# Layer 1's feed-forward: the second half's norm steps and the down weights' splits at other products of a tile

## The chip, the core and the metric

One core of a Trainium2 chip runs the whole program. The metric is the device time of one execution in microseconds. In the profile PE is the matrix engine (TensorE), DVE VectorE, ACT ScalarE, POOL GpSimd, and SP the engine that here only issues DMA transfers.

## What is computed

A two-layer block over 1024 latent tokens and 256 context tokens of width 1024, in float32. Layer 0 mixes by Fourier groups and windowed attention, layer 1 by neighbourhood attention; each layer ends with a SwiGLU feed-forward. Cut to the part that matters here, layer 1's end:

```
o = _neighbourhood_attention(q, k, v, kc, vc, rel_bias) @ w_out
x = x + g1 * o
h = _rms(x, norm2_g[i]) * (1.0 + sc2) + sh2
x = x + g2 * ((jax.nn.silu(h @ wg) * (h @ wu)) @ wd)     # D_FF = 2816
```

## The kernel before

Every float32 product is made of three matmuls on parts: an operand is split into a high part (rounded) and a low part (the rest), and `mm3` (lines 74 to 76) adds high x high, high x low and low x high. ACT makes a high part by a copy, POOL or DVE the low part by a subtraction. These splits, not only the matmuls, fill the other engines.

Layer 1's feed-forward works on two halves of 512 tokens. The 2816 hidden columns are 22 tiles of 128 (`NF`), so there are 44 tiles (`NT1`): n = 0 to 21 for the first half, 22 to 43 for the second. In a tile the gate and up products are computed together as seven block products (`p`, s = 0 to 6, lines 1451 to 1495) over four combinations of the weights' blocks; `sums1` makes the combinations on POOL (tile `t`, line 1400), `high1` and `low1` split them (lines 1413, 1417, 1425), five to seven products ahead of their use. DVE and ACT combine the seven results (lines 1466 to 1484), ACT makes `act_hi` (line 1489) and POOL `act_lo` (line 1492). Products with the down weights (`d`, `down_product`, line 1497) take two tiles' `act` at once: eight of them, for tiles n and n+1 with n even, stand four in tile n+2 and four in tile n+3, behind s = 2, 4, 5 and 6. The order of all these items is a list, `items`, and on PE, DVE, ACT and POOL every instruction runs in the order of the program (`manual_schedule`). SP is not in that list; its order is chosen by the compiler's planner.

The input of a half is normed ahead of its tiles. For the first half this is done by `norm0s` during the out projection. For the second half `norm1s` (a generator, line 1300) does it during the tiles of the first half: each `advance(own1, 1)` runs it to its next `yield`. It makes eight squares on ACT (line 1308) with sums on POOL (line 1309), a chain by two groups of small matmuls with Ln and Exp between them (lines 1313 to 1322), and then, for four pairs of columns blocks, `own` tiles: a product on POOL (line 1327) and a scale on ACT (1328) for each of the two, differences on POOL (1330 to 1334), and four pieces that are split by ACT (`own_hi`, 1339) and POOL (1340) and leave by DMA for the buffer `c_d` in HBM. `own_hi` has one buffer. In tile 21 the parts come back from `c_d` on SP's queue, and tile 22 reads them.

`split_down(n, h, t)` splits half h of the down weights of tile n: t = 0 is ACT's copy (line 1444), t = 1 POOL's subtraction (line 1446). `load_down(n + 1)` at s=5 of tile n loads both halves into `wd_raw`, which has three buffers (line 1436). What steps run behind which product is written out at the end of the loop over `items`.

Of the kernel before, what the change touches and what calls it, by code (L numbers as in the profile page):

```python
# [27 lines left out]
NF = DFF // P  # L28
# [27 lines left out]
def bc(ap, axis, n):  # L56

    ap = ap.unsqueeze(axis)
    shape = list(ap.shape)
    shape[axis] = n  # L60
    return ap.broadcast_to(shape)


def build(tc, io):
    nc = tc.nc
# [3 lines left out]
    def fl(ap):  # L69
        return ap.bitcast(F32)  # L70
# [7 lines left out]
    def rsqrt_into(r, v, tmp):  # L78

        S.activation(r, v, AF.Ln)  # L80
        S.activation(r, r, AF.Exp, scale=-0.5)
        V.tensor_tensor(tmp, r, r, ALU.mult)
        V.scalar_tensor_tensor(tmp, v, -0.5, tmp, ALU.mult, ALU.mult)
        V.scalar_tensor_tensor(r, tmp, 1.5, r, ALU.add, ALU.mult)
# [27 lines left out]
    def vec(l, which):  # L112
        return mod[l][:, which * KT:(which + 1) * KT, :]
# [36 lines left out]
    def advance(steps, n):  # L150

        for _ in range(n):
            if next(steps, steps) is steps:
                return
# [90 lines left out]
    def product(c, u, k, out, c0, n):  # L245
        ts = slice(u * P, u * P + P)
        mm3(out, hs[c][0][:, k, ts], hs[c][1][:, k, ts], w_hi[:, k, c0:c0 + n], w_lo[:, k, c0:c0 + n],
            k == 0, k == KT - 1)
# [100 lines left out]
    for c in range(T // CH):  # L349
        h_hi, h_lo = hs[c]  # L350

        for u in range(CH // P):
# [34 lines left out]
            for i, h0, nh in ((0, 0, 8), (1, 8, 2)):  # L387
                src = pqf[:, h0 * HD:(h0 + nh) * HD]
# [83 lines left out]
    for half in range(2):  # L472
# [5 lines left out]
        for gg in range(2):  # L478
# [3 lines left out]
            for i0, parts in ((0, (0, 4)), (2, (1, 2)), (4, (3,))):  # L482
# [8 lines left out]
                n = len(parts)  # L491
                src = ps[:, 0:n].rearrange("p n r l -> p r n l")
# [25 lines left out]
    for grp in range(4):  # L518
# [5 lines left out]
        src = ps.rearrange("p n r l -> p r n l")  # L524
# [703 lines left out]
    HT = 256  # L1228
# [71 lines left out]
    def norm1s():  # L1300

        ss = wk.tile([P, 512], F32, name="nrm_ss")
        for k in range(KT):
            if k == 0:
                S.activation(ss, x[:, k, 512:], AF.Square)
            else:
                sq = wk.tile([P, 512], F32, name="nrm_sq", tag="nrm_r")
                S.activation(sq, x[:, k, 512:], AF.Square)
                G.tensor_tensor(ss, ss, sq, ALU.add)
            yield  # L1310
        ps = ph.tile([P, 512], F32, name="pmisc")
        for j in range(4):
            TE.matmul(ps[:, j:j + 1], ss[:, j * P:(j + 1) * P], ones[:, 0:1], start=True, stop=True)
        v = wk.tile([P, 3, 4], F32, name="nrm_v", bufs=2)
        S.activation(v[:, 0], ps[:, :4], AF.Identity, bias=eps, scale=1.0 / D)
        rsqrt_into(v[:, 1], v[:, 0], v[:, 2])
        yield
        ps = ph.tile([P, 512], F32, name="pmisc")
        for j in range(4):
            TE.matmul(ps[:, j * P:(j + 1) * P], bc(v[:, 1, j], 1, P), ident, start=True, stop=True)  # L1320
        r = wk.tile([P, 512], F32, name="nrm_r")
        S.copy(r, ps)
        yield
        for i in range(4):
            h0, h4, s_, r_ = (wk.tile([P, 512], F32, name="own", bufs=4) for _ in range(4))
            for k, h in ((i, h0), (i + 4, h4)):
                G.tensor_tensor(h, x[:, k, 512:], r, ALU.mult)  # L1327
                S.activation(h, h, AF.Identity, bias=vec(1, 3)[:, k, 0:1], scale=nA[3][:, k, 0:1])  # L1328
                yield
            G.tensor_tensor(s_[:, M1], h0[:, M2], h4[:, M2], ALU.add)  # L1330
            G.tensor_tensor(s_[:, M2], s_[:, M1], h0[:, M1], ALU.subtract)
            yield
            G.tensor_tensor(r_[:, M1], h0[:, M1], h0[:, M2], ALU.subtract)
            G.tensor_tensor(r_[:, M2], h4[:, M1], s_[:, M2], ALU.subtract)
            yield
            for sl, src in ((slice(0, 1), h0[:, M1]), (slice(1, 3), h4), (slice(3, 5), s_), (slice(5, 7), r_)):
                n = (sl.stop - sl.start) * HT
                hi = wk.tile([P, 512], F32R, name="own_hi", tag="nrm_ss")
                S.copy(hi[:, :n], src)
                G.tensor_tensor(src.bitcast(F32R), src, fl(hi[:, :n]), ALU.subtract)  # L1340
                yield
                for t, part in ((0, fl(hi[:, :n])), (1, src)):
                    nc.scalar.dma_start(c_d[:, sl, t, i], part.rearrange("p (a n) -> p a n", n=HT))
                yield


# [22 lines left out]
    NT1 = 2 * NF  # L1369
# [19 lines left out]
    def sums1(q):  # L1389

        n, s = divmod(q, 7)
        if n >= NT1:
            return
        d = tiles[n]
        b11, b12, b22, b21 = d["b"]
        which = {0: ("t1", b12, b11), 1: ("t2", b22, d.get("t1")), 2: ("t3", b22, b12), 4: ("t4", d.get("t2"), b21)}
        if s in which:
            name, a, b = which[s]
            d[name] = wk.tile([P, 4, P], F32, name=name, tag="t", bufs=4)
            G.tensor_tensor(d[name], a, b, ALU.subtract)  # L1400

    def high1(q):

        n, s = divmod(q, 7)
        if n >= NT1:
            return
        if s == 0 and n + 1 < NT1:
            load_tile(n + 1)
        d = tiles[n]
        b11, b12, b22, b21 = d["b"]  # L1410
        src = (b11, d.get("t2"), d.get("t3"), d["t1"], d.get("t4"), b21, b22)[s]
        hi, lo = (ww.tile([P, 4, P], F32R, name=m) for m in ("w_hi", "w_lo"))
        S.copy(hi, src)  # L1413
        first = fl(hi)
        if s < 6:
            first = ph.tile([P, 512], F32, name="pmisc").rearrange("p (k n) -> p k n", n=P)
            S.copy(first, fl(hi))  # L1417
        d["w"][s] = hi, lo, src, first

    def low1(q):  # L1420
        n, s = divmod(q, 7)
        if n >= NT1:
            return
        hi, lo, src, first = tiles[n]["w"][s]
        (V if s < 6 else G).tensor_tensor(lo, src, first, ALU.subtract)  # L1425
# [4 lines left out]
    c_d = tc.dram_tile([P, 7, 2, 4, HT], F32, name="c_d")  # L1430
    down_raw = {}

    def load_down(n):
        for h in range(2):
            raw = wk.tile([P, 4, P], F32, name="wd_raw", bufs=3)
            nc.sync.dma_start(raw, io["w_down"][1, n % NF][:, 4 * h:4 * h + 4])
            down_raw[n, h] = raw

    def split_down(n, h, t):

        f = n % NF
        parts = [w_room[n // 2 % 2][:, f % 2, h, i] for i in range(2)]
        if t == 0:
            S.copy(parts[0], down_raw[n, h])
        else:
            G.tensor_tensor(parts[1], down_raw.pop((n, h)), fl(parts[0]), ALU.subtract)  # L1446
# [50 lines left out]
    def down_product(n, dt):  # L1497
        ci, f = divmod(n, NF)
        w_in = w_room[n // 2 % 2]
        ts = slice(ci * 512, ci * 512 + 512)  # L1500
        ps = pd.tile([P, 512], F32, name="d_ps")
        for i in range(2):
            mm3(ps, w_in[:, i, dt // 4, 0, dt % 4], w_in[:, i, dt // 4, 1, dt % 4], *tiles[n + i]["act"],
                i == 0, i == 1)
        V.scalar_tensor_tensor(x[:, dt, ts], ps, vec(1, 5)[:, dt, 0:1], x[:, dt, ts], ALU.mult, ALU.add)  # L1505
        if f == NF - 2:
            nc.scalar.dma_start(io["out"][:, dt, ts], x[:, dt, ts])
# [18 lines left out]
    with tc.manual_schedule(engines={E.PE, E.DVE, E.Activation, E.Pool}):  # L1526
        for i, (kind, n, s) in enumerate(items):
            for step in later.pop(i, ()):
                step()
            if kind == "d":  # L1530
                down_product(n, s)
                continue
            q = 7 * n + s
            sums1(q + LEAD + 2)
            if q:
                low1(q + LEAD - 1)
            high1(q + LEAD)
            product(i, n, s)
            if s == 5 and n + 1 < NT1:
                load_down(n + 1)  # L1540
            if q == 0:
                load_down(0)
            if s in (3, 4):
                split_down(n, 0, s - 3)
            if s in (0, 1) and n:
                split_down(n - 1, 1, s)
            if n == NT1 - 1 and s > 4:
                split_down(n, 1, s - 5)
            if 0 < n < NF - 1 and s in (0, 2, 4, 6):
                advance(own1, 1)  # L1550
            if n == NF - 1:

                for t, dst in ((0, c_hi), (1, c_lo)):
                    nc.sync.dma_start(fl(dst[:, SLOTS[s]]), c_d[:, SLOTS[s], t])
        for i in sorted(later):
            for step in later[i]:
                step()
# [113 lines left out]
```

## Time and profile before

| | us |
|---|---|
| median of 3 runs | 2896.84 |
| lowest and highest of them | 2896.06 and 2900.75 |
| the profiled execution | 2901.23 |
| its span | 2899.4 |

The profiled execution is 4.4 us above the median of the runs, and 1.8 us of its time lie outside the span. In the timeline a line gives the start in us from the span's beginning, the duration, engine, line and operation, and in brackets the time the engine stood idle before it with what ended the wait. Matmuls overlap, so one of 0.28 us follows another after 0.12 us.

### The profile page before, as it was taken

The numbers are of one execution on the slowest core, as the hardware profiler recorded it, in microseconds if no ns is written. First come the engines' busy times: TensorE is split into PE (matmuls) and PEld (weight loads), VectorE is DVE, ScalarE is ACT, GpSimd is POOL, SyncE is SP. The second block draws the span as 40 slices with busy tenths as digits, with TensorE's granted clock in tenths as the row PEclk, the third lists the DMA queues.
The fourth block names the chain that finished last, engine by engine and source line by source line (L and its number), as shares of the span: only waits on it lengthen the run. The fifth ranks groups of instructions, "written<-read, shape, count | busy, mean of one in ns | idle before, by whom it ended". The sixth has DMA issues, their size and how long they took to land. (4 is left out here: it accounts for less than half of the span.)

```text
span 2899.4 us, 44678 instructions
## 1 busy us (share of the span) xinstructions
PE 2799.8 (97%) x16874; PEld 2346.2 (81%) x16874; DVE 1510.4 (52%) x3069; ACT 1214.7 (42%) x2402; POOL 825.3 (28%) x857
## 2 busy tenths in 40 slices
PE   7988999999999999999989999999998999999999
PEld 5876767888888888888867788777777888999998
DVE  5775553533223333333377243366556676666665
ACT  4345553421111111111154232466637677666664
POOL 1122332000000000000040000355427788666664
PEclk9988999999999999999999999999999999999999
DMA  7235655211011011011124333877354344363331
GB/s 281 76 125 215 220 217 160 73 37 41 33 37 44 30 44 44 30 44 36 38 87 137 104 109 110 197 180 167 95 163 137 113 133 144 106 240 103 105 103 70
DMA packets 162375, 321.10 MB, mean 111 GB/s; under 512 B 13904, under 2 KB 78928, under 8 KB 155120
## 3 DMA queue, kind: packets, MB, share of 16 engines
q1 hardware_dynamic: 147200, 294.05, 32.4%
q10 hardware_dynamic: 13008, 15.87, 1.5%
q0 software_dynamic: 1952, 8.32, 1.0%
q8 instruction: 134, 2.20, 0.3%
q14 instruction: 81, 0.66, 0.1%
HBM read 269.83 MB, written 48.37 MB: 110 GB/s over the span
## 5 line engine op out<-in xcount | busy, mean ns | idle before, releaser
L74 PE MATMUL p_ps<-c_hi,w_hi 128*128 128x256 f32 x1232 | 343.6, 279 | 3.1 <-ACT own L1328 1.5
L76 PE MATMUL p_ps<-c_hi,w_lo 128*128 128x256 f32 x1232 | 342.2, 278 | 1.6 <-DVE w_lo L1425 1.0
L75 PE MATMUL p_ps<-c_lo,w_hi 128*128 128x256 f32 x1232 | 342.1, 278 | 0.0
L810 POOL TENSOR_TENSOR nrm_ss<-nrm_ss,nrm_sq 128x512 f32<-128x512 f32 (+1 forms) x31 | 39.3, 1269 | 1011.9 <-PE d_ps L76 935.7
L775 ACT CAST w_hi<-w_raw 128x1024 fp32r<-128x1024 f32 x106 | 110.3, 1050 | 482.5 <-PE d_ps L75 270.5
L74 PEld LDWEIGHTS p_ps<-c_hi,w_hi 128*128 128x128 f32 x1232 | 233.0, 189 | 12.3 <-ACT pmisc L1417 1.5
L75 PEld LDWEIGHTS p_ps<-c_lo,w_hi 128*128 128x128 f32 x1232 | 232.9, 189 | 6.8
L76 PEld LDWEIGHTS p_ps<-c_hi,w_lo 128*128 128x128 f32 x1232 | 232.7, 189 | 2.2 <-DVE w_lo L1425 1.5
L580 POOL TENSOR_SCALAR pr<-pr,st 128x640 f32<-128x640 f32 (+2 forms) x208 | 156.7, 754 | 267.1 <-DVE st L579 177.3
L878 DVE SCALAR_TENSOR_TENSOR x<-d_ps,mod,x 128x512 f32<-128x512 f32 (+1 forms) x240 | 157.5, 661 | 125.3 <-PE d_ps L76 125.3
L776 DVE TENSOR_TENSOR w_lo<-w_raw,w_hi 128x1024 fp32r<-128x1024 f32 x102 | 124.1, 1223 | 183.3 <-ACT w_hi L775 180.9
L862 DVE TENSOR_TENSOR sg<-sg,u_ps 128x512 f32<-128x512 f32 (+1 forms) x66 | 39.5, 599 | 319.9 <-PE u_ps L76 319.9
L1505 DVE SCALAR_TENSOR_TENSOR x<-d_ps,mod,x 128x512 f32<-128x512 f32 x176 | 132.1, 751 | 127.0 <-PE d_ps L76 126.4
L74 PE MATMUL d_ps<-act_hi,w_hi 128*128 128x512 f32 (+1 forms) x528 | 189.3, 359 | 3.4 <-DVE x L878 3.4
L75 PE MATMUL d_ps<-act_lo,w_hi 128*128 128x512 f32 (+1 forms) x528 | 189.2, 358 | 1.3 <-DVE act_lo L864 1.3
L76 PE MATMUL d_ps<-act_hi,w_lo 128*128 128x512 f32 (+1 forms) x528 | 189.2, 358 | 0.0
L74 PE MATMUL u_ps<-o_hi,w_hi 128*128 128x512 f32 (+1 forms) x528 | 188.3, 357 | 0.0
L75 PE MATMUL u_ps<-o_lo,w_hi 128*128 128x512 f32 (+1 forms) x528 | 188.3, 357 | 0.0
L76 PE MATMUL u_ps<-o_hi,w_lo 128*128 128x512 f32 (+1 forms) x528 | 188.3, 357 | 0.0
L74 PE MATMUL g_ps<-o_hi,w_hi 128*128 128x512 f32 (+1 forms) x528 | 188.3, 357 | 0.0
L75 PE MATMUL g_ps<-o_lo,w_hi 128*128 128x512 f32 (+1 forms) x528 | 188.2, 357 | 0.0
L76 PE MATMUL g_ps<-o_hi,w_lo 128*128 128x512 f32 (+1 forms) x528 | 188.2, 357 | 0.0
(332 smaller groups left out, 7456.9 us busy)
## 6 DMA issues: line engine op xcount, KB each, us to landing
ada_w<-ada_w SPq DMA_DIRECT2D x48, 1024.0 KB, 4.9
wd_raw<-w_down SPq DMA_DIRECT2D x88, 256.0 KB, 2.6
w_raw<-w_gate SPq DMA_DIRECT2D x88, 256.0 KB, 3.0
w_raw<-w_up SPq DMA_DIRECT2D x88, 256.0 KB, 2.9
k<-k_d SPq DMA_DIRECT2D x28, 640.0 KB, 10.6
w_raw<-w_in SPq DMA_DIRECT2D x24, 512.0 KB, 4.0
w_raw<-w_gate SPq DMA_DIRECT2D x22, 512.0 KB, 3.5
w_raw<-w_up SPq DMA_DIRECT2D x22, 512.0 KB, 3.5
```

The lines of the kernel that those rows point to most:

```text
L74: TE.matmul(out, lh, rh, start=first, stop=False)
L75: TE.matmul(out, lh, rl, start=False, stop=False)
L76: TE.matmul(out, ll, rh, start=False, stop=last)
L580: G.tensor_scalar(self.pr[:, :n], self.pr[:, :n], st[:, 3:4], 0.0, ALU.mult, ALU.add)
L775: S.copy(hi, raw)
L776: eng.tensor_tensor(lo, raw, fl(hi), ALU.subtract)
L810: adder(i).tensor_tensor(ss, ss, sq, ALU.add)
L862: V.tensor_tensor(sg[:, :n], sg[:, :n], u_ps[:, :n], ALU.mult)
L878: V.scalar_tensor_tensor(xs, self.shaped(ps[:, :n]), vec(l, 5)[:, dt, v:v + 1], xs, ALU.mult, ALU.add)
L1505: V.scalar_tensor_tensor(x[:, dt, ts], ps, vec(1, 5)[:, dt, 0:1], x[:, dt, ts], ALU.mult, ALU.add)
```

## The change

Three edits. The steps of `norm1s` start at tile 3 instead of tile 1 and stand at s = 3, 5 and 6 instead of 0, 2, 4 and 6. The down weights are split at other products: the first half of tile n at s = 5 and 6 of that tile (before: 3 and 4), the second half at s = 3 and 4 of tile n+1 (before: 0 and 1), and for the last tile behind its last product. In `norm1s` a piece of `own` is split and sent in one step instead of two, and its second (low) part is issued on SP's queue instead of ACT's.

```
-                yield
-                for t, part in ((0, fl(hi[:, :n])), (1, src)):
-                    nc.scalar.dma_start(c_d[:, sl, t, i], part.rearrange("p (a n) -> p a n", n=HT))
+                for t, part, q in ((0, fl(hi[:, :n]), nc.scalar), (1, src, nc.sync)):
+                    q.dma_start(c_d[:, sl, t, i], part.rearrange("p (a n) -> p a n", n=HT))
                 yield
...
-            if s in (3, 4):
-                split_down(n, 0, s - 3)
-            if s in (0, 1) and n:
-                split_down(n - 1, 1, s)
-            if n == NT1 - 1 and s > 4:
-                split_down(n, 1, s - 5)
-            if 0 < n < NF - 1 and s in (0, 2, 4, 6):
+            if s in (3, 4) and n:
+                split_down(n - 1, 1, s - 3)
+            if s > 4:
+                split_down(n, 0, s - 5)
+            if q == 7 * NT1 - 1:
+                for t in range(2):
+                    split_down(n, 1, t)
+            if 2 < n < NF - 1 and s in (3, 5, 6):
                 advance(own1, 1)
```

## Rows read from the trace of the kernel before

**Rows 1.** The head of the page, part 1: busy time of the matrix engine, its share of the span, and its instructions.

```profile
PE 2799.8 (97%) x16874; PEld 2346.2 (81%) x16874; DVE 1510.4 (52%) x3069; ACT 1214.7 (42%) x2402; POOL 825.3 (28%) x857
```

**Rows 2.** Busy time by stretch. Columns: start and end, length, then for each engine its busy time with the number of instructions in brackets, the granted clock, the busy share of the DMA engines and their rate. The stretches are the tiles 0 and 1 of the block product with the first columns of tile 2, the tiles over which `norm1s` is stepped, and the rest up to the last tile.

```profile
2196.00:2233.00 37.00, 27.82 (x212) 25.35 (x211) 22.20 (x41) 33.38 (x62) 30.95 (x25) 0.95 0.41 133
2233.00:2455.00 222.00, 210.55 (x1460) 193.94 (x1459) 149.31 (x257) 151.69 (x281) 177.71 (x149) 0.98 0.39 126
2455.00:2870.00 415.00, 415.00 (x2966) 386.51 (x2965) 284.35 (x524) 281.87 (x526) 277.07 (x220) 1.00 0.38 125
```

**Rows 3.** Single matmuls of the timeline ahead of which PE stood still: start, duration, and in the brackets at the end the idle time before it with what ended it.

```profile
2227.78 0.49 PE L74 MATMUL d_ps<-act_hi,h_hi 128*128 128x512 f32 x1 [1.96 <-ACT act_hi L1489]
...
2232.30 0.79 PE L75 MATMUL d_ps<-act_lo,h_hi 128*128 128x512 f32 x1 [4.02 <-POOL act_lo L1492]
...
2251.70 1.16 PE L1320 MATMUL pmisc<-ident,nrm_v 128*128 128x128 f32 x8 [1.81 <-DVE w_lo L1425]
...
2304.40 0.80 PE L75 MATMUL d_ps<-act_lo,h_hi 128*128 128x512 f32 x1 [3.60 <-POOL act_lo L1492]
...
2337.86 0.50 PE L75 MATMUL d_ps<-act_lo,h_lo 128*128 128x512 f32 x1 [1.43 <-POOL act_lo L1492]
...
2367.39 0.35 PE L74 MATMUL p_ps<-c_hi,w_hi 128*128 128x256 f32 x1 [1.32 <-ACT own L1328]
...
2370.50 0.50 PE L75 MATMUL d_ps<-act_lo,h_hi 128*128 128x512 f32 x1 [0.51 <-POOL act_lo L1492]
...
2401.83 0.50 PE L75 MATMUL d_ps<-act_lo,h_lo 128*128 128x512 f32 x1 [0.82 <-POOL act_lo L1492]
...
2434.37 0.50 PE L75 MATMUL d_ps<-act_lo,h_hi 128*128 128x512 f32 x1 [1.63 <-POOL act_lo L1492]
...
2884.94 0.50 PE L75 MATMUL d_ps<-act_lo,h_lo 128*128 128x512 f32 x1 [0.79 <-POOL act_lo L1492]
```

**Rows 4.** Three stretches that were granted the lower clock, and one of the same length as the third behind it; columns as in group 2, PE alone.

```profile
2229.20:2236.00 6.80, 3.70 (x15) 0.50 0.26 84
2253.10:2256.50 3.40, 3.40 (x13) 0.50 0.46 155
2304.30:2307.70 3.40, 3.30 (x13) 0.50 0.30 101
2307.70:2311.10 3.40, 3.40 (x26) 1.00 0.62 180
```

**Rows 5.** Timeline of PE: the first matmul of the last block product (`p_ps`), and of the down product behind it (`d_ps`).

```profile
2880.29 0.28 PE L74 MATMUL p_ps<-c_hi,w_hi 128*128 128x256 f32 x1
...
2881.66 0.39 PE L74 MATMUL d_ps<-act_hi,h_hi 128*128 128x512 f32 x1
```

**Rows 6.** Busy time in one whole tile behind the stretch of `norm1s`; columns as in group 2.

```profile
2490.40:2505.50 15.10, 15.10 (x110) 14.07 (x109) 10.23 (x20) 10.26 (x21) 10.08 (x8) 1.00 0.33 106
```

**Rows 7.** Timeline of the three other engines ahead of the wait that ended at 2304.40: start, duration, engine, line, operands, idle time before it with its end.

```profile
2292.22 4.24 DVE L1480 TENSOR_TENSOR av<-av,u 128x256 f32<-128x256 f32 x1
...
2292.36 1.31 POOL L1446 TENSOR_TENSOR h_hi<-wd_raw,h_hi 128x512 fp32r<-128x512 f32 x1
...
2294.87 1.31 POOL L1400 TENSOR_TENSOR t<-w_raw 128x512 f32<-128x512 f32 x1
...
2300.37 0.36 ACT L1466 COPY p<-p_ps 128x256 f32<-128x256 f32 x1
...
2301.15 0.62 ACT L1339 CAST own_hi<-own 128x512 fp32r<-128x512 f32 x1
...
2301.84 1.27 POOL L1340 TENSOR_TENSOR own<-own,own_hi 128x512 fp32r<-128x512 f32 x1 [5.67 <-ACT own_hi L1339]
2303.07 1.27 POOL L1492 TENSOR_TENSOR act_lo<-av,act_hi 128x512 fp32r<-128x512 f32 x1
```

**Rows 8.** Busy time of POOL in the stretch of `norm1s`, first for the instructions on tile `own`, then for those on `nrm_ss`; columns: start, end, length, POOL's busy time (instructions), clock, DMA share, rate.

```profile
2210.00:2455.00 245.00, 41.62 (x40) 0.97 0.39 126
...
2210.00:2455.00 245.00, 8.97 (x7) 0.97 0.39 126
```

**Rows 9.** Busy time between two `act_lo`, those of tiles 0 and 1; columns as in group 2. Then from the timeline the `act_hi` of tile 1.

```profile
2215.10:2230.90 15.80, 10.18 (x76) 8.84 (x74) 7.93 (x15) 14.85 (x29) 15.06 (x13) 0.95 0.36 115
...
2227.13 0.61 ACT L1489 CAST act_hi<-av 128x512 fp32r<-128x512 f32 x1
```

**Rows 10.** DMA issues between 2196 and 2460: the first half of a split part leaving for `c_d`, count, KB each, median us from issue to landing.

```profile
c_d<-own_hi ACTq DMA_DIRECT2D x12, 256.0 KB, 2.2
```

**Rows 11.** Timeline of the norm's chain: ACT's read of the sums, and the last of the three small DVE steps.

```profile
2247.02 0.27 ACT L1315 ACTIVATE nrm_v<-pmisc,eps 128x4 f32<-128x4 f32 x1
...
2250.88 0.16 DVE L84 SCALAR_TENSOR_TENSOR nrm_v<-nrm_v 128x4 f32<-128x4 f32 x1
```

**Rows 12.** Timeline at the end of the kernel: the first DVE step behind the last block product, POOL's last split and its last `act_lo`.

```profile
2881.87 0.42 DVE L1483 TENSOR_TENSOR u<-p_ps,u 128x256 f32<-128x256 f32 x1 [0.62 <-PE p_ps L76]
...
2877.81 1.30 POOL L1446 TENSOR_TENSOR h_lo<-wd_raw,h_lo 128x512 fp32r<-128x512 f32 x1 [3.54 <-ACT h_lo L1444]
...
2883.61 1.28 POOL L1492 TENSOR_TENSOR act_lo<-av,act_hi 128x512 fp32r<-128x512 f32 x1 [4.50 <-ACT act_hi L1489]
```

**Rows 13.** All 44 products of line 1480: durations in ns as min/median/max, first and last start, shape.

```profile
L1480 DVE TENSOR_TENSOR av<-av,u x44: 415/416/4235, 2209.2 to 2879.4; 128x256 f32<-128x256 f32 x44
```

**Rows 14.** Waits of the SP queue, 2260 to 2460: the loads of the down weights, what they waited for, us in total, times, longest.

```profile
SPq L1436 <- POOL h_hi L1446: 39.4, 12, 5.4
```

## The prediction, made before the change was run

> **What bounds the kernel now.** I read the page's head first: PE is busy for 97% of the span [rows 1]. Next I cut the last part of the kernel into stretches. Behind the tiles in which `norm1s` is stepped, from 2455 to 2870, PE is busy for all of 415 us [rows 2]: there no order of other engines' work can win anything, it can only lose. The two stretches ahead of it do hold idle time, 37.00 - 27.82 = 9.2 us and 222.00 - 210.55 = 11.4 us. So I looked up each matmul ahead of which PE stood [rows 3]. In tile 2 it waited 1.96 us for `act_hi` and 4.02 for `act_lo` of tile 1. Then 1.81 us for the norm's small chain. Then five times for `act_lo` of an odd tile, at the first down product of the next even tile, 3.60 + 1.43 + 0.51 + 0.82 + 1.63 = 7.99 us, and once 1.32 behind an `own` step of ACT. Together 17.1 us. The rest in the first stretch lies ahead of the code that is changed. One more wait of 0.79 us stands at the very end.
>
> Idle time is not the whole price. In or right behind the waits of 4.02, 1.81 and 3.60 us PE was granted the lower clock, 1.2 GHz [rows 4]: 13 matmuls in 3.4 us where the next 3.4 us, at 2.4 GHz, hold 26. The three stretches have 3.70 + 3.40 + 3.30 = 10.4 us of work at half speed, so 5.2 us lost. Behind the waits of 1.63 us and less the clock did not fall.
>
> All that the change can give back is thus 17.1 + 5.2 = 22.3 us.
>
> **The clock of a tile.** A product or a down product takes 1.37 us [rows 5]; a tile from the third on has seven and four, 11 x 1.37 = 15.1 us. Behind the steps of `norm1s` a tile took exactly that, with POOL busy for 10.08 us in 8 instructions [rows 6], 1.26 each. `act_lo` of an odd tile is needed by the fourth matmul of the first down product of the next tile. That is, counted from the end of its last product: one down product, three products, 0.7 us for three matmuls of that down product and some 0.2 for the one before it, 4 x 1.37 + 0.9 = 6.4 us.
>
> **Why `act_lo` is late now.** It stands on POOL behind the `own` step of s=0. That step needs ACT's `own_hi`, and ACT does this behind the copy of the product s=0, which needs the product's end. The wait of 3.60 us shows the chain without a gap [rows 7]: the copy at 2300.37, `own_hi` to 2301.77, `own` from 2301.84, `act_lo` to 2304.34, 4.0 us behind the copy's start. The copy can't start before 2 x 1.37 = 2.7 us of the 6.4 are gone, so even a tile with nothing else late ends at 6.7 and waits 0.3 us. What is more than that in the five waits is delay from a full POOL.
>
> **Edit 1: no `norm1s` step ahead of n=3, and steps at s=3, 5, 6.** The steps do 41.62 + 8.97 = 50.6 us of POOL work [rows 8]. There were 59 calls at four a tile, 14.8 tiles, 3.4 us in each; now (16 yields fewer) 43 calls at three, 14.3 tiles, 3.5 us. POOL then has 10.1 + 3.5 = 13.6 of 15.1 us: it fits as before. They end in tile 17, far ahead of tile 21, which reads `c_d` back.
>
> (a) Tile 1. Between `act_lo` of tile 0 and of tile 1 POOL was busy for 15.06 of 15.80 us and ACT for 14.85 [rows 9]. Twelve POOL instructions start there: four are sums of `norm1s` and go; the split of (1, second half) goes behind `act_lo`; one of (0, second half) comes in. Eight are left, 8 x 1.26 = 10.1 us, 5.7 less. ACT loses four squares and a split's copy at 14.85 / 29 = 0.51 us, 2.6 us, so `act_hi` comes at 2224.5 instead of 2227.13, and POOL can begin `act_lo` at about 2225.2 and end at 2226.5. PE without its first wait asks for it at 2232.30 - 4.02 - 1.96 = 2226.3. I take 5.0 of 5.98 us as won (bounds 3 and 5.98).
>
> (b) The norm's chain. From ACT's read to DVE's last step it takes 2251.04 - 2247.02 = 4.0 us [rows 11]. Its two halves were two products apart, 2.7 us; now they are s=6 and s=3 of the next tile, six pieces or 8.2 us. The 1.81 us go. But the chain now stands ahead of an odd tile's last DVE product: 1.0 us of small matmuls, 4.0, then 0.4 + 0.7 + 1.3 for the product, `act_hi` and `act_lo` are 7.4 us, with 6.4 + 1.0 allowed. It just fits; a wait of 0 to 2 us there is in (c).
>
> (c) Tiles 3 to 16. `own` of s=6 needs `own_hi` of s=6, and that tile's buffer is free only when the piece of s=5 has left: 2.2 us to landing [rows 10]. The two steps are two pieces, 2.7 us, apart, and the issue takes about 0.4 more, so ACT does `own_hi` some 1 us behind the last product's end. Then POOL does `own`, `t` for the next tile and `act_lo`, 3 x 1.26 = 3.8: 4.9 us of 6.4. The five waits and the 1.32 go, 9.3 us; for seven odd tiles I leave 0.3 us each, 2.3 with (b)'s, and count 7.0 (bounds 4 and 9.3).
>
> (d) The clock. Two of the three falls should go with the waits they followed. I leave one of the short ones, 1.7 of 5.2 us, since (b) and (c) may hold a wait of that size: 3.5 (bounds 1.7 and 5.2).
>
> **Edit 2: the splits.** They stay 88 on ACT and 88 on POOL. In a tile without `norm1s` the copies go from s=0 and 1 to s=3 and 5, POOL's share to s=4 and 6. POOL has 15.1 - 10.1 = 5 us free in such a tile [rows 6]; both halves are split a tile or more ahead of the down products that read them, save the first half of an odd tile, ready some 6 us ahead. Nothing is won or lost. With one cost: three raw buffers serve two loads a tile, so SP's second load now waits for the split at s=6, not that at s=4, about 4 us later. SP waits there already for 39.4 us in 12 times [rows 14] and PE never for it; what is queued behind it on SP are the loads of a tile used more than ten us later. At the last tile two splits fall on s=6. Now POOL's last split runs at 2877.81 and `act_lo` at 2883.61 [rows 12]: 4.5 us idle between, room for both. The 0.79 us stay.
>
> **Edit 3: the second part leaves by SP.** ACT gives up 16 issues and the wait for POOL ahead of each; SP takes them. Cover as for edit 2; I count nothing, between a loss of 1 us (a load behind a late `own`) and a gain of 1.
>
> **The sum.** 5.0 + 1.8 + 7.0 + 3.5 = 17.3 us. The profiled execution took 2901.23, so 2883.9; the median of the runs is 4.4 below it, so 2879.5. By the bounds of the four terms: 22.3 us, 2874.5, to 3 + 1.3 + 4 + 1.7 = 10 us, 2887.
>
> **The rivals.** *DVE shut out by POOL (slower).* One DVE product with two SBUF operands, line 1480, took 4.24 us while POOL ran three instructions end to end, 2292.36 to 2296.18 [rows 7]; the median of the 44 is 0.416 [rows 13]. The change puts two `own` steps and a split on POOL at s=5 and 6, where this product and the next stand, and `act_hi` is behind them. If POOL has no gap there, each odd tile 5 to 15 costs what the wait of 2304.40 cost, 3.60 and the slow clock's 1.65: 6 x 5.25 = 31.5, less what (a), (b), the first clock fall (1.85) and the removed 9.3 and 1.65 give, 19.6: 12 us slower, 2909. It decides from 19.6 / 6 = 3.3 us a tile. Against it: `own` of s=6 waits for a landing, which leaves POOL a gap of about 1 us, enough for a product of 0.42. The Trainium skill (SBUF — State Buffer, "SBUF: two separate sides") says that VectorE and GpSimd share a port pair under an exclusive lock held for a whole instruction, a DVE operation with two SBUF inputs among those that lock out. The row of 4.24 us agrees with it.
>
> *The waits of tiles 3 to 16 only move.* (c) and its fall give nothing: 5.0 + 1.8 + 1.85 = 8.7 us, 2888. For it: POOL's load per tile is the same.
>
> *The change does not do what it says.* In tiles 0 and 1, without down products, a tile is 7 x 1.37 = 9.6 us, and POOL's eight instructions alone need 10.1. If that, not `norm1s`, makes tile 1 late, (a) stays, and with (c) unchanged only 1.8 us go: 2895, no change. Against it: the excess is 0.5 us a tile, the wait 5.98.
>
> **How the numbers follow.** Runs of this kernel lie within some 0.2% (5.8 us), which I take as the bound of no change. The forecast has 0.62, between 2874 and 2887; waits that only move 0.16; no effect 0.10; shut out 0.12. The predicted time is the forecast's. The range runs from 2871 to 2894: it takes in the forecast, the rival of 2888 and a part of no effect, and leaves out the slower rival. Faster 0.78, same 0.10, slower 0.12.
>
> **What would show it.** In the changed kernel's profile: (a) no wait over 1 us for `act_hi` or `act_lo` in tile 2; (b) none ahead of line 1320; (c) waits of `d_ps` for `act_lo` under 3 us in sum ahead of the last tile; (d) at most one stretch at the lower clock behind the first product. Wrong would be: long products on lines 1480 and 1484 with `act_lo` waits behind them, POOL waiting for raw loads, or idle PE behind 2455.

## The result, and the profile after

| | before | after |
|---|---|---|
| median, us (four runs each, on one chip) | 2898.80 | 2879.61 |
| lowest and highest | 2896.06, 2901.50 | 2877.20, 2880.66 |
| the profiled execution, its span | 2901.23, 2899.4 | 2877.20, 2875.4 |

The changed kernel is faster by 19.2 us: the ratio of the times is 0.993, with a 95% interval of 0.9919 to 0.9942. In a later job on one chip, with more runs of both, the medians were 2883.67 and 2899.38, 15.7 us apart (ratio 0.9945, 0.9933 to 0.9957). The prediction was 17.3 us less than before, 2879.5.

One of the executions used below, the profiled one of e_act, took 5794 us, twice as long as every other, and is left out of its median.

The two profiled executions differ by more, 24.0 us, since that of before was at the slower end of its runs and that of after the fastest of its own. To compare traces I use one length throughout: from PE's wait inside the first product of layer 1's feed-forward (the wait of `p_ps` at 2199 in before and 2198 in after) to the last `act_lo` wait at the kernel's end. Stretches at the lower clock in layer 0 differ from one execution to the next and fall outside this length. It was 2884.94 - 2199.02 = 685.92 us before and 2860.93 - 2198.18 = 662.75 after: 23.2 us gone. Below this length is called the stretch.

Line numbers from 1341 on are one lower in after: 1480 is 1479, 1484 is 1483, 1492 is 1491.

The head of after's page, part 1, beside [rows 1]:

```profile
PE 2790.6 (97%) x16874; PEld 2340.8 (81%) x16874; DVE 1520.6 (53%) x3069; ACT 1218.4 (42%) x2402; POOL 830.6 (29%) x857
```

Busy time by stretch in after, columns as in [rows 2] (the third ends earlier, since the kernel does):

```profile
2196.00:2233.00 37.00, 33.05 (x254) 30.93 (x253) 27.82 (x51) 33.15 (x62) 29.78 (x25) 1.00 0.45 150
2233.00:2455.00 222.00, 221.35 (x1584) 205.75 (x1583) 155.66 (x278) 170.25 (x314) 195.26 (x162) 1.00 0.40 135
2455.00:2850.00 395.00, 395.00 (x2821) 367.80 (x2820) 283.75 (x496) 268.40 (x493) 268.54 (x209) 1.00 0.37 125
```

In the first two stretches PE was idle for 3.95 and 0.65 us, where before it was 9.2 and 11.4 [rows 2]. The clock is 1.00 in all three: no fall is left, where before there were three [rows 4]. The same 222 us hold 124 matmuls more. POOL is busier in the second stretch, 195.26 against 177.71 us: all sums of `norm1s` now stand in it (9.69 us on `nrm_ss` against 3.86), and more of the tiles' own work fits into it. PE does not wait for it there.

All of PE's waits from 2185 to the end in after; columns: who waited, for whom, us in total, times, the longest:

```profile
PE d_ps L75 <- POOL act_lo L1491: 2.1, 2, 1.3
PE p_ps L76 <- DVE w_lo L1424: 1.1, 1, 1.1
PE p_ps L74 <- ACT p L1465: 0.9, 2, 0.7
PE p_ps L76 <- POOL w_lo L1424: 0.4, 1, 0.4
PE pmisc L1320 <- DVE w_lo L1424: 0.5, 1, 0.5
PE pmisc L1313 <- DVE w_lo L1424: 0.2, 1, 0.2
```

The waits of the timeline that are left, beside [rows 3]: in tile 2, at the norm's chain, and at the end.

```profile
2225.45 0.50 PE L75 MATMUL d_ps<-act_lo,h_hi 128*128 128x512 f32 x1 [1.34 <-POOL act_lo L1491]
...
2290.09 1.16 PE L1320 MATMUL pmisc<-ident,nrm_v 128*128 128x128 f32 x8 [0.49 <-DVE w_lo L1424]
...
2860.93 0.50 PE L75 MATMUL d_ps<-act_lo,h_lo 128*128 128x512 f32 x1 [0.79 <-POOL act_lo L1491]
```

Of the ten waits of [rows 3] three are left: 1.34 in place of 1.96 + 4.02, 0.49 in place of 1.81, and the 0.79 at the end. The five at odd tiles' `act_lo` and the 1.32 behind `own` are gone.

### The profile page after: what moved, and what is told of

It reads as the page before. It is cut to its first block, busy times and chain, and to the rows that moved or that the text cites. A ratio compares the mean times of both kernels' runs of the same rounds, so it can differ in the third digit from the quotient of the medians.

```text
span 2875.4 us, 44686 instructions
## 1 busy us (share of the span) xinstructions
PE 2790.6 (97%) x16874; PEld 2340.8 (81%) x16874; DVE 1520.6 (53%) x3069; ACT 1218.4 (42%) x2402; POOL 830.6 (29%) x857
```

## The experiments

Each job ran its kernels and the kernel before on one chip. "Waits" are PE's waits behind 2210 with the 0.79 at the end; "low clock" is the time in the stretch at 1.2 GHz. Stretch, waits and low clock come from one execution of each kernel, the median from all. Executions of one kernel lie up to 11 us apart (2894.14 to 2905.09 for before in one job), so the median and its ratio tell what a kernel is worth, and the other columns tell where. Times and waits in us.

| kernel | stretch | waits | low clock | median | before | ratio (95%) |
|---|---|---|---|---|---|---|
| before | 685.9 | 19.5 | 13.7 | | | |
| after | 662.8 | 3.4 | 0 | 2879.61 | 2898.80 | 0.993 (0.9919 to 0.9942) |
| after_again | 662.5 | 3.5 | 0 | 2883.67 | 2899.38 | 0.9945 (0.9933 to 0.9957) |
| e_start | 679.8 | 16.0 | 6.8 | 2898.40 | 2900.19 | 0.9993 (0.9984 to 1.0002) |
| e_0246 | 684.0 | 15.4 | 17.1 | 2898.86 | 2900.19 | 0.9994 (0.9985 to 1.0003) |
| e_0246_gap | 665.6 | 5.9 | 0 | 2885.37 | 2899.38 | 0.9947 (0.9936 to 0.9959) |
| e_035 | 667.7 | 7.3 | 0 | 2884.44 | 2902.01 | 0.9948 (0.9935 to 0.9962) |
| e_234 | 670.8 | 8.5 | 3.4 | 2884.82 | 2902.01 | 0.9949 (0.9937 to 0.9962) |
| e_3456 | 671.0 | 9.3 | 3.4 | 2889.76 | 2902.01 | 0.9967 (0.9956 to 0.9979) |
| e_split | 663.9 | 4.8 | 0 | 2882.26 | 2900.19 | 0.9944 (0.9932 to 0.9957) |
| e_merge | 686.7 | 18.8 | 20.5 | 2903.02 | 2902.01 | 1.0007 (0.9998 to 1.0015) |
| e_act | | | | 2881.01 | 2900.19 | 0.9934 (0.9921 to 0.9948) |
| e_act_2 | 665.6 | 5.6 | 0 | 2883.01 | 2899.38 | 0.9941 (0.9929 to 0.9952) |
| e_low_end | 662.6 | 3.5 | 0 | 2881.30 | 2899.38 | 0.9942 (0.993 to 0.9954) |

The theory at the start was the prediction's: the later start relieves tile 1 (a), the steps' places relieve tiles 3 to 16 because no `own` stands at s=0 (c). The rivals on record were that the places within a tile alone matter, and that the splits' places or SP's issue bring the gain.

**e_start: before, with the steps from tile 3 on and nothing else changed.**

```
-            if 0 < n < NF - 1 and s in (0, 2, 4, 6):
+            if 2 < n < NF - 1 and s in (0, 2, 4, 6):
```

> The kernel before with one thing changed: the steps of norm1s start at tile 3; they stay at s=0, 2, 4, 6, and the splits, the two-step split of a piece and both issues on ACT stay as they were. Theory (POOL and ACT work ahead of act_lo of tile 1 makes tile 2 wait; own at s=0 makes the later tiles wait; the clock falls follow the waits): the two waits of tile 2, 5.98 us, fall to 1 to 2, and the fall of the clock there goes, 1.85; the norm's 1.8 and the waits of later tiles, some 8 to 9, stay: 6 to 7 us faster than before, about 2892. Rival (only the places within a tile matter): no change, 2898.

The wait in tile 2 fell as told, from 5.98 to 1.45 us, and the medians show no gain: 1.8 us, with an interval from 4.6 us faster to 0.6 slower. The expectation of 6 to 7 us missed. The rival's number came out, but not its reason, since tile 2 did change. Part of what was won was given back: the norm's chain waited 4.01 us instead of 1.81 and the clock fell in that wait (6.8 us at 1.2 GHz in one stretch), and `act_lo` was late eight times, 8.7 us in all with tile 2's 1.45 and the end's 0.79. The one traced execution has a stretch 6.1 us shorter than before's, as the theory had it; why the medians do not show that much stays open. PE's two waits:

```profile
2228.02 0.50 PE L75 MATMUL d_ps<-act_lo,h_hi 128*128 128x512 f32 x1 [1.45 <-POOL act_lo L1492]
...
2279.83 2.07 PE L1320 MATMUL pmisc<-ident,nrm_v 128*128 128x128 f32 x8 [4.01 <-DVE w_lo L1425]
```

And DVE and POOL ahead of the second one:

```profile
2276.25 0.49 DVE L82 TENSOR_TENSOR nrm_v<-nrm_v 128x4 f32<-128x4 f32 x1 [4.92 <-ACT nrm_v L81]
2276.77 1.19 DVE L83 SCALAR_TENSOR_TENSOR nrm_v<-nrm_v 128x4 f32<-128x4 f32 x1
2278.00 1.19 DVE L84 SCALAR_TENSOR_TENSOR nrm_v<-nrm_v 128x4 f32<-128x4 f32 x1
...
2275.44 1.28 POOL L1446 TENSOR_TENSOR h_hi<-wd_raw,h_hi 128x512 fp32r<-128x512 f32 x1
2276.67 1.27 POOL L1400 TENSOR_TENSOR t<-w_raw 128x512 f32<-128x512 f32 x1
2277.89 1.27 POOL L1425 TENSOR_TENSOR w_lo<-w_raw,w_hi 128x512 fp32r<-128x512 f32 x1
2279.11 1.28 POOL L1400 TENSOR_TENSOR t<-t,w_raw 128x512 f32<-128x512 f32 x1
```

The `pmisc` buffer that PE writes is given free by a `w_lo` behind these steps on DVE. Three DVE steps on four columns took 0.49, 1.19 and 1.19 us, where the last took 0.16 before [rows 11]. Each ends with a POOL instruction that ran beside it: 2.87 us for what is 0.48 us at 0.16 each, 2.4 us more. That is about as much as the wait grew, 2.20.

**e_0246: after, with four steps a tile at the old places.**

```
-            if 2 < n < NF - 1 and s in (3, 5, 6):
+            if 2 < n < NF - 1 and s in (0, 2, 4, 6):
```

> The changed kernel with the steps back at s=0, 2, 4, 6 (start at tile 3, splits, one-step pieces and SP's issue stay changed). Theory: tile 2 stays as in the changed kernel (one wait of about 1.3 us), the norm's 1.8 come back, and act_lo of the odd tiles waits again behind own of s=0, 5 to 9 us in sum, with one or two falls of the clock, 1.7 to 3.4: 2888 to 2893. Rival (the splits' places or SP's issue bring the gain): 2880.

The old places with four steps a tile take back the whole gain, more than the theory allowed. Tile 2 waited 1.36 us, as in after, so (a) holds whatever the places are. The loss stands in later tiles, where PE waits twice in each of three down products, and the clock falls. One of them in the timeline, first what POOL, ACT and DVE do:

```profile
2394.15 1.29 POOL L1327 TENSOR_TENSOR own<-x,nrm_r 128x512 f32<-128x512 f32 x1
2395.47 0.82 ACT L1328 ACTIVATE own<-own,mod,nA 128x512 f32<-128x512 f32 x1 [3.73 <-POOL own L1327]
2396.20 0.40 ACT L1475 ACTIVATE u<-u 128x256 f32<-128x256 f32 x1
2396.63 0.43 DVE L1479 TENSOR_TENSOR av<-av,u 128x256 f32<-128x256 f32 x1 [3.76 <-ACT u L1475]
...
2401.12 0.81 ACT L1328 ACTIVATE own<-own,mod,nA 128x512 f32<-128x512 f32 x1 [1.39 <-POOL own L1327]
2401.84 0.60 ACT L1488 CAST act_hi<-av 128x512 fp32r<-128x512 f32 x1
...
2402.28 0.73 POOL L1330 TENSOR_TENSOR own<-own 128x256 f32<-128x256 f32 x1
2403.09 0.72 POOL L1331 TENSOR_TENSOR own<-own 128x256 f32<-128x256 f32 x1
2403.77 1.27 POOL L1491 TENSOR_TENSOR act_lo<-av,act_hi 128x512 fp32r<-128x512 f32 x1
```

Then PE behind them:

```profile
2402.50 0.49 PE L74 MATMUL d_ps<-act_hi,h_lo 128*128 128x512 f32 x1 [1.27 <-ACT act_hi L1488]
...
2405.10 0.80 PE L75 MATMUL d_ps<-act_lo,h_lo 128*128 128x512 f32 x1 [2.11 <-POOL act_lo L1491]
```

A step asks POOL for the product of `own` (1327) and sets ACT to its scale (1328) at once. POOL's queue is full, so the product runs late, and ACT, which works in order, stands for 3.73 us. Behind ACT stands the `u` of the feed-forward (1475), behind `u` DVE's product (1479, idle for 3.76 us for it), then `act_hi`, then `act_lo`, then PE. Between `act_hi` and `act_lo` POOL also does the two `own` differences of s=0 (1330, 1331); `act_lo` starts 1.3 us behind the end of `act_hi`. So the new theory was: what costs is ACT standing at 1328, not POOL's work itself.

These are not the waits of before come back. There a piece of `own` took two steps and a round of `norm1s` (one pair of column blocks) twelve, three tiles long. With edit 3 a round has eight steps, two tiles at four a tile, so each round stands at the same products: both `own` products at s=4 and 6 of the odd tiles 5, 7, 9 and 11, and no piece at s=0 of an even tile.

**e_0246_gap: e_0246, with ACT's scale one step behind POOL's product.** This takes the suspected wait away and keeps the steps at s=0, 2, 4 and 6, but a round then has ten steps.

```
                     G.tensor_tensor(...)      # line 1327, own
+                    yield
                     ...                       # line 1328, ACT's scale of own
```

> The changed kernel with four steps a tile at s=0, 2, 4, 6 (as the run before with these places), and one edit more: a yield between POOL's product and ACT's scale of an own tile, so that ACT scales it one step after POOL was asked for it. Theory (four steps a tile cost because ACT stands at the scale until POOL's full queue has come to the product, 18.6 us in 8 waits there, and DVE's products and act_hi stand behind ACT): ACT's wait for that product falls under 5 us, the waits of PE in tiles 6 to 12 (10.9 us with two long stretches at the lower clock) fall to 2 to 5, and the time to 8 to 14 us below the run without the gap, 2885 to 2891. Rival (steps at s=0 or four steps a tile cost by POOL's load alone): 2895 to 2900 as before.

ACT's wait at its scale, first in e_0246, from 2196 to 2460:

```profile
ACT own L1328 <- POOL own L1327: 18.6, 8, 4.6
```

and in e_0246_gap, where the scale is line 1329:

```profile
ACT own L1329 <- POOL own L1327: 0.2, 1, 0.2
```

With 18.4 us of ACT's waits the stretch lost 18.5 us, every lower clock in it, and of PE's waits behind tile 2 all but 0.47, 0.44 and the norm's 1.86. The kernel is as fast as after within the intervals, at the old places, and its time is the theory's. Two things move along. With 8 more yields the steps, four to a tile, fill 51 / 4 = 12.75 tiles instead of 43 / 4 = 10.75, so POOL's side work is 50.6 / 12.75 = 4.0 us a tile instead of 4.7. And other steps stand at the products: in e_0246 tiles 7, 9 and 11 each hold two pieces and both `own` products; in e_0246_gap no odd tile holds pieces and an `own` product together. The two traces show ACT's wait on the way to PE, and that it is gone; how much of the 18.5 us is the gap's and how much the other order's was not separated.

**e_035 and e_234: after, with other three places.** The prediction put the waits down to the `own` step at s=0, so one kernel keeps a step there; the other has three steps in a row and none at s=0.

```
-            if 2 < n < NF - 1 and s in (3, 5, 6):
+            if 2 < n < NF - 1 and s in (0, 3, 5):
```

> The changed kernel with the steps at s=0, 3, 5: three a tile, one of them at s=0. Theory of the place: own or its scale at s=0 stands ahead of act_lo again, 0.3 to 2 us in each of six or seven odd tiles and one to three falls of the clock, 2884 to 2893. Rival (the number of steps a tile decides, four having been too many): as the changed kernel, 2879 to 2882.

```
+            if 2 < n < NF - 1 and s in (2, 3, 4):
```

> The changed kernel with the three steps at s=2, 3, 4 instead of 3, 5, 6: as many steps a tile, right behind act_lo instead of ahead of it. Theory of the place (what costs is a step that stands on POOL or ACT between the last products and the next act_lo, above all at s=0): no waits in the later tiles, as in the changed kernel, 2878 to 2883. Rival (the steps have to be late in the tile): waits of d_ps for act_lo in the odd tiles, 2886 to 2895.

The two are alike, and most of the gain is there in both. The time of e_035 is at the low end of its range, with waits in four tiles and no fall of the clock; that of e_234 lies above the theory's range and below the rival's. In e_035 the waits for `act` behind tile 2 are 0.92, 0.21, 0.56 and 0.73 us, 2.4 in sum. The first stands behind a sum of squares at s=0 of tile 4, the others behind a piece of `own` at s=0 of tiles 8, 14 and 16; no other even tile has a piece there, and none waits for `act`. So the prediction's mechanism for (c) is there. POOL in tiles 14 and 16, the piece and `act_lo` behind it:

```profile
2414.02 1.29 POOL L1340 TENSOR_TENSOR own<-own,own_hi 128x512 fp32r<-128x512 f32 x1 [0.53 <-ACT own_hi L1339]
2415.26 1.28 POOL L1491 TENSOR_TENSOR act_lo<-av,act_hi 128x512 fp32r<-128x512 f32 x1
...
2445.25 1.30 POOL L1340 TENSOR_TENSOR own<-own,own_hi 128x512 fp32r<-128x512 f32 x1 [3.03 <-ACT own_hi L1339]
2446.51 1.27 POOL L1491 TENSOR_TENSOR act_lo<-av,act_hi 128x512 fp32r<-128x512 f32 x1
```

In e_234, without a step at s=0, two waits for `act_lo` are left behind tile 2, 0.90 and 0.64 us, and others for the sums, for `u` and for `w_hi`, up to 1.37. Its ACT stood at 1328 for 16.6 us in 7 times, nearly as long as in e_0246, and PE waited 4.2 us in all of that part of the kernel (0.43 + 0.90 + 1.37 + 0.64 + 0.37 + 0.49). So ACT's wait costs by what stands behind it at that product, not by its length.

**e_3456: after, with four steps a tile at late products.**

```
+            if 2 < n < NF - 1 and s in (3, 4, 5, 6):
```

> The changed kernel with four steps a tile, at s=3, 4, 5, 6. Theory of the place: none at s=0, so waits for act_lo stay small, up to 0.5 us in an odd tile; POOL has up to 5.5 us more than its 10.1 in a tile, which is over 15.1 in some: 2880 to 2886. Rival (the number of steps a tile decides): 2890 to 2899, as with s=0, 2, 4, 6.

Between the theory's range and the rival's (2890 to 2899), at the edge of the latter. ACT's wait at 1328 is short, 3.0 us, so the late places avoid that one also with four steps. The losses are others: the norm's chain waited 3.11 us, since its two halves now are one product apart (with two products apart, in e_0246, it is 1.65: 1.46 less, about the 1.37 of a product), and ACT stood for 13.7 us, in 6 times, ahead of `own_hi` for the departure of the piece before it.

**e_split: after, with the down weights' splits at their old products.**

```
-            if s in (3, 4) and n:
-                split_down(n - 1, 1, s - 3)
-            if s > 4:
-                split_down(n, 0, s - 5)
-            if q == 7 * NT1 - 1:
-                for t in range(2):
-                    split_down(n, 1, t)
+            if s in (3, 4):
+                split_down(n, 0, s - 3)
+            if s in (0, 1) and n:
+                split_down(n - 1, 1, s)
+            if n == NT1 - 1 and s > 4:
+                split_down(n, 1, s - 5)
```

> The changed kernel with the splits of the down weights back at their old products. Theory: one POOL instruction and one ACT copy more stand ahead of act_lo of tile 1, so the wait in tile 2 grows from 1.34 to 2.5 or 3 us; the other tiles stay without waits: 2881 to 2883. Rival (the splits at s=0 and 1 were what made act_lo late): the waits of odd tiles come back, 2886 to 2890.

The wait in tile 2 grew to 1.45 us only, not to 2.5 or 3, with 0.96 for `w_lo` ahead of it (0.41 in after). The stretch is 1.1 us longer than after's, the ratio the same within the intervals. In the traces edit 2 is worth about 1 us, at these places of the steps; the old places of the steps were not run with edit 2 alone.

**e_act and e_act_2: after, with the second part leaving on ACT's queue again.** The first gives a time alone, the second, of the same kernel, also a trace.

```
-                for t, part, q in ((0, fl(hi[:, :n]), nc.scalar), (1, src, nc.sync)):
+                for t, part, q in ((0, fl(hi[:, :n]), nc.scalar), (1, src, nc.scalar)):
```

> The changed kernel with the second part of a piece issued on ACT's queue again, in the same step as the first. Theory: ACT has to wait for POOL's subtraction at each of 16 pieces, but is idle for a quarter of the time and its weights are five products ahead: 0 to 2 us slower than the changed kernel, 2880 to 2882. Rival (freeing ACT is what brings the gain): act_hi comes late, waits of PE for act_hi or act_lo in tiles 7 to 16, 2885 to 2890.

> The changed kernel with the second part of a piece on ACT's queue again, once more for its profile. Theory: ACT waits for POOL at 16 pieces, some 1 us each, and PE for at most 2 us more than in the changed kernel; 0 to 2 us slower than it. Rival: waits of PE for act_hi or act_lo in tiles 7 to 16, 5 us and more.

The medians show no difference. In the trace ACT stood for the low part of `own` for 7.4 + 6.9 + 3.6 = 17.9 us, and of that PE saw four waits of 0.33 to 0.85 us; the stretch is 3 us longer. So the queue of edit 3 may be worth up to 3 us, less than these medians resolve.

**e_merge: before, with edit 3 alone** (the first part of the diff at the head of this document).

> The kernel before with edit 3 alone: a piece is split and sent in one step, its second part by SP; start at tile 1, steps at s=0, 2, 4, 6 and the old splits stay. Theory: the places that cost are unchanged, the waits stay in tile 2 and in fewer later tiles (43 calls end in tile 11), with heavier steps: 2893 to 2902. Rival (one-step pieces and a freer ACT bring the gain): 2885 to 2890.

No gain, 1 us above the theory's range: the waits in tile 2 are still 1.97 + 4.01 us. Those of later tiles are as long in sum, 8.9 us, but they are others. As in e_0246 a round is two tiles long and both `own` products stand at s=4 and 6 of an odd tile; ACT stood there for 16.0 us in 4 times, and PE behind it:

```profile
2301.52 0.36 PE L74 MATMUL p_ps<-c_hi,w_hi 128*128 128x256 f32 x1 [2.55 <-ACT own L1328]
...
2336.15 0.55 PE L74 MATMUL p_ps<-c_hi,w_hi 128*128 128x256 f32 x1 [3.32 <-DVE u L1482]
...
2371.83 0.36 PE L74 MATMUL p_ps<-c_hi,w_hi 128*128 128x256 f32 x1 [2.55 <-ACT own L1328]
```

**e_low_end: after, with `act_lo` of tiles 0 and 1 one product earlier, and the last one on DVE.** This goes for what after still has: 1.34 us in tile 2 and 0.79 at the end.

```
-            after(3 if n < NT1 - 1 else 2, act_low)
+            after(3 if 1 < n < NT1 - 1 else 2, act_low)
...
-                G.tensor_tensor(d["act"][1], avf, fl(d["act"][0]), ALU.subtract)
+                (G if n < NT1 - 1 else V).tensor_tensor(d["act"][1], avf, fl(d["act"][0]), ALU.subtract)
```

> The changed kernel with two edits of act_lo: for tiles 0 and 1 it is issued one product earlier, ahead of one combination on POOL, and for the last tile it is done by DVE instead of POOL. Theory: the wait of 1.34 us in tile 2 falls to 0 to 0.3, the one at the end from 0.79 to 0.6: 1 to 1.5 us faster than the changed kernel beside it, less than the runs can tell apart. Rival (tile 2 is late for another reason): its wait stays above 1 us.

The wait in tile 2 went from 1.56 (in after_again, the same job) to 0.85, between theory and rival, but two waits ahead of it grew from 0.22 and 0.29 to 0.56 and 0.91; the end's fell from 0.78 to 0.52. Stretch and time are those of after.

**after_again: after once more, in the same job as e_low_end.**

> The changed kernel itself, beside the others on the same chip: 19 to 20 us below the kernel before, waits of PE behind 2210 of some 3.4 us in sum.

Its median is 15.7 us below before's, less than the 19 to 20 expected. Its waits, 3.5 us in sum, and its stretch are as in after.

## Why the prediction was right

The sum, term by term, in the profiles:

| term | predicted | measured |
|---|---|---|
| (a) `act` of tile 1 | 5.0 | 5.98 - 1.34 = 4.6 |
| (b) the norm's chain | 1.8 | 1.81 - 0.49 = 1.3 |
| (c) tiles 3 to 16 | 7.0 | 7.99 + 1.32 - 0 = 9.3 |
| (d) the clock | 3.5 | 5.2 - 0 = 5.2 |
| sum | 17.3 | 20.4 |

The stretch lost 23.2. The other 2.8 us the sum left out: 0.9 us of waits under 1 us, which stand in tiles 1 and 2 for the most part, and matmuls that run slower just behind a wait, some 0.27 us for each. The medians gave 19.2 and 15.7. The forecast lies between these two, the profiles' 23.2 above both, since single executions scatter.

*(a)* was right in place and, within 0.4 us, in size, and the wait's fall is shown: e_start has it alone (5.98 to 1.45). Its sign, no wait over 1 us in tile 2, was not met. POOL's part came as forecast: counted from the start of the stretch, which lies 0.84 us earlier in after, `act_lo` ended where the forecast had it, within 0.3 us (2225.40 + 0.84 = 2226.2, forecast 2226.5). PE was there earlier, at 2225.45 - 1.34 + 0.84 = 2224.9 instead of 2226.3. The prediction set the other waits of the first stretch aside as lying ahead of the changed code; four of them, 1.3 us, lie in tiles 1 and 2, behind the first steps, and in after 0.6 us is left of these.

```profile
2224.13 1.27 POOL L1491 TENSOR_TENSOR act_lo<-av,act_hi 128x512 fp32r<-128x512 f32 x1
```

*(b)* was nearly right in size, though its sign, no wait ahead of line 1320, was missed by 0.49 us, and its working is borne out with one link more. From the first group of small matmuls to the second it took 2279.34 - 2273.73 = 5.6 us in e_0246 with 1.65 us of it open, and the same 5.6 in e_3456 with 3.11 open; in after the two are 10.0 us apart, and the chain's last DVE step ended 5.1 us ahead of the second group:

```profile
2280.06 1.02 PE L1313 MATMUL pmisc<-ones,nrm_ss 128*128 128x1 f32 x8 [0.16 <-DVE w_lo L1424]
...
2284.85 0.16 DVE L84 SCALAR_TENSOR_TENSOR nrm_v<-nrm_v 128x4 f32<-128x4 f32 x1
```

The link that the prediction left out is the one that the row names. The second group writes a `pmisc` buffer, and DVE's `w_lo` (line 1425 before, 1424 after) has to have read it. In before that `w_lo` stood on DVE behind the chain's three steps, which had kept DVE idle for 4.58 us:

```profile
2250.36 0.29 DVE L82 TENSOR_TENSOR nrm_v<-nrm_v 128x4 f32<-128x4 f32 x1 [4.58 <-ACT nrm_v L81]
...
2250.96 0.68 DVE L1425 TENSOR_TENSOR w_lo<-w_raw,pmisc 128x512 fp32r<-128x512 f32 x1
```

It ended at 2251.64, and PE began at 2251.70. So of the 1.81 us the chain itself held PE to 2251.04, 1.15 us, and the `w_lo` behind it 0.66. In after the `w_lo` that gives the buffer free is a later one, which ends at 2290.04, with the chain long done. That is the 0.49 that is left, and in e_035 the 2.05, where the chain was done 3.8 us before.

*(c)* was under-sized (7.0 for 9.3; I had left 2.3 us of waits, and there is none). Its reason holds: in before each of the five waits stands behind an `own` step at s=0, four of them, 7.5 of the 9.3 us, behind a piece that POOL splits right ahead of `act_lo` [rows 7 for the first]. The other three:

```profile
2335.29 1.30 POOL L1340 TENSOR_TENSOR own<-own,own_hi 128x512 fp32r<-128x512 f32 x1 [3.56 <-ACT own_hi L1339]
2336.54 1.26 POOL L1492 TENSOR_TENSOR act_lo<-av,act_hi 128x512 fp32r<-128x512 f32 x1
...
2399.24 1.30 POOL L1340 TENSOR_TENSOR own<-own,own_hi 128x512 fp32r<-128x512 f32 x1 [2.38 <-DVE u L1468]
2400.49 1.28 POOL L1492 TENSOR_TENSOR act_lo<-av,act_hi 128x512 fp32r<-128x512 f32 x1
...
2431.81 1.29 POOL L1340 TENSOR_TENSOR own<-own,own_hi 128x512 fp32r<-128x512 f32 x1 [2.40 <-ACT own_hi L1339]
2433.05 1.26 POOL L1492 TENSOR_TENSOR act_lo<-av,act_hi 128x512 fp32r<-128x512 f32 x1
```

The start of `act_hi` and of `act_lo`, in us behind the end of the tile's last product. PE waits when `act_lo` starts later than 5.1 (in tile 5 of after 6.3, since the norm's first matmuls stand in between); in after it did not wait in any of these:

| tile | before: `act_hi` | before: `act_lo` | PE waited | after: `act_hi` | after: `act_lo` |
|---|---|---|---|---|---|
| 5 | 4.27 | 8.67 | 3.60 | 5.53 | 6.23 |
| 7 | 2.08 | 6.51 | 1.43 | 2.12 | 2.82 |
| 11 | 1.32 | 5.89 | 0.82 | 4.15 | 4.83 |
| 13 | 2.29 | 6.71 | 1.63 | 2.69 | 4.79 |

With a piece at s=0, `act_lo` comes 4.4 to 4.6 us behind `act_hi`; where POOL has nothing between, 0.7. At 0.7 none of the four would have waited. In e_035 the same way takes 3.9 us, since the copy of the down weights' split, which in before stands on ACT between the two, has left s=0 with edit 2. e_start has the same steps in other tiles and nearly the same waits: 0.97, 1.61, 0.83 and 1.58.

What was wrong in the prediction's reading is the rest, which it called "delay from a full POOL": POOL stood idle ahead of each of these steps, for 5.67 [rows 7], 3.56, 2.38 and 2.40 us. It waited for ACT's `own_hi`, which stands on ACT behind `act_hi`, and `act_hi` was late, most of all in tile 5, behind the DVE product of 4.24 us [rows 7]. In e_start, where that line's longest product is 1.62 us, the same place costs 0.97 instead of 3.60.

The last 1.8 us, 1.32 + 0.51 in tile 10, are of e_0246's kind: ACT had stood for 3.78 us at the scale of `own` in tile 9, and the feed-forward's `u` stands behind it. The same wait of ACT in the even tiles 6 and 12 cost PE at most 0.16. In after ACT waits there more often, but not as long, and none of it reaches PE:

```profile
ACT own L1328 <- POOL own L1327: 7.7, 6, 2.1
```

In before these were 11.3 us in 3 times. The new places leave little room: in tile 11 `act_lo` starts 0.2 to 0.3 us before PE would wait. Why s = 3, 5 and 6 do better than 2, 3 and 4 was not worked out: e_234 has 8.0 us of stretch more than after, with 16.6 us of such waits of ACT, and e_035 4.9 us with 5.9.

*(d)* was under-sized in the same way: I left one fall, none came, as no wait behind the first product is over 1.34 us; but other runs show falls behind waits as short (last section), so that is no proof.

*Edits 2 and 3 at nothing*: borne out, within about 1 us (e_split) and within 3 (e_act_2, e_merge), as far as these runs resolve.

*The rivals.* "The waits only move" is what e_start did at the old places; in e_0246 other waits took the place of before's. The new places, or the gap with its other order, got out of it. The new places with the old start were not run. "No effect" fell with (a). "DVE shut out by POOL" is there in the trace of after and costs PE nothing: the split at s=6 now runs beside line 1479, whose median rose from 0.416 [rows 13] to 1.107 us (0.417 in e_split, with the splits at their old products).

```profile
L1479 DVE TENSOR_TENSOR av<-av,u x44: 412/1107/1583, 2207.8 to 2855.4; 128x256 f32<-128x256 f32 x44
```

Its longest is 1.58, no longer 4.24, and no PE wait follows. 0.7 us a tile is far from the 3.3 from which the rival decided. The Trainium skill (SBUF — State Buffer, "SBUF: two separate sides") has the lock of the port pair held for a whole instruction; the trace agrees as far as it shows: in e_start two steps of four columns each took 1.19 us and ended with a POOL instruction of 1.27, and 1.107 less 0.416 us leaves 0.69 of waiting, less than one such instruction. In the row of 4.24 us [rows 7] three of them ran end to end beside it.

## What to carry to other kernels

When a side job is stepped through a full schedule, issue what an in-order engine does with another engine's product one step behind the request; otherwise that engine stands for the other's queue, and what it costs is set by who stands behind it. When the number of steps changes, look again at which step stands at which product: e_0246 and e_merge had before's places and other waits. Test the parts of a reordering alone and together: here the later start removed the longest wait and alone gave no gain that the medians show; with other places for the steps it gave 0.6%. Take the releaser that a row names literally before looking past it: the norm's wait named `w_lo`, and it was `w_lo`, held up by the chain ahead of it on DVE.

## What the runs showed of the hardware that was not expected

A DVE operation on 128x4 elements, 0.16 us alone, took 0.49, 1.19 and 1.19 us in e_start while POOL ran 1.27-us instructions end to end. I had watched only the large products for this; in a chain of small steps it cost up to 1.0 us per step, and here it turned a wait of 1.81 into one of 4.01.

A wait's length did not tell what the clock would do. The prediction read from before that behind waits of 1.63 us and less it did not fall [rows 3, 4]. In e_234 it fell to 1.2 GHz behind a wait of 1.37 us, ahead of the norm's one-column matmuls, and in e_3456 behind two of 0.81 and 0.84 in one down product, while behind the 3.11 us of e_3456 and the 2.05 of e_035 it stayed at 2.4 GHz. The falls took 3.4 to 10.2 us each (the longest in tile 2 of e_merge); after had none.
